# One weight sum per Strassen pair made by an accumulating DMA, splits of weights given priority, plain matmuls moved into the first pair, and y_diag issued ahead of the state update

## The chip, the cores and the metric

The kernel runs on one core of one Trainium2 chip. The metric is the device time of one execution in microseconds (us). The time before is the median of three runs. One further execution was taken with the hardware profiler; every share, row and duration below is from that one.

## The reference

One Mamba-2 layer on 512 tokens of 2048 channels, then a final RMSNorm. Everything is float32.

```python
hn   = rmsnorm(x, ln_g)                         # 512 x 2048
proj = hn @ w_in                                # 2048 x 10304: z 4096, xBC 6144, dt 64
xbc  = silu(causal_depthwise_conv(xBC))         # x 4096, B 8 x 128, C 8 x 128
dt   = softplus(dt + dt_bias);  a = -exp(a_log)
# per head (64 heads of 64 channels, 8 groups of 8 heads share B and C):
#   y_diag = (C B^T * decay) (x dt);  y_off = C state exp(cs);  state update
y    = (ssd_scan(x * dt, dt * a, B, C) + D * x) * silu(z)
out  = rmsnorm(x + rmsnorm(y) @ w_out, final_g)
```

## The kernel before

**Exact products from rounded parts.** TensorE's fast format is float32r. Each weight piece of 128 x 1024 floats (512 KB) is loaded raw and split by `split_piece` (L84): ScalarE casts it to a float32r part `hi` (L87), VectorE subtracts to make the rest `lo` (L88). The input `xh`, `xl` is split once. A product of k-slices is three matmuls: hi*xh, hi*xl, lo*xh (L635, L636, L637 for the in projection; L867, L868, L869 and L929, L930, L931 for the out projection).

**Plain part.** A head section computes dt from its weights, and eight 128-channel tiles (B0, C0 and the first x and z tiles) are multiplied in the plain way (`mm_k`, L198): 16 k-slices of three 512-column matmuls.

**Quads.** The other 36 pairs of tiles (`quads`: an x tile with its z tile, or a B tile with its C tile) go through `pair` (L639): one 2 x 2 Strassen-Winograd step with seven products of 24 matmuls of 128 x 256 each instead of eight. The weights of the products are, in the order in which a regular pair multiplies them, R11, T1, (T4 of the pair before), T2, R22, R21, T3. R11, R12, R21, R22 are quarters as loaded. T1 = R11 + another quarter and T3 = R12 + another are formed by an accumulating DMA on GpSimd's queue (`q_fetch`, L595, issue at L598): the second quarter is added into the raw piece in place. T2 = T1 + R22 and T4 = T2 + R21 are formed by VectorE in place (`q_add`, L604, 128 x 1024). The chain R11, T1, T2, T4 lives in one raw buffer of `ra` (three of them), R12 and T3 in the single `rb`, R22 and R21 in the two `rc`; the float32r parts rotate through three pairs of buffers, those of R11 have a pair of their own (`h1h`, `h1l`).

**The scan.** For each of 32 units (two heads), small groups of matmuls are inserted between the products: transposes (`u_xt`), the state update (`u_state`, L488), y_diag (`u_yd`, L502 and L506) and y_off (`u_yo`, L520). Between them ScalarE makes the decay exponentials (`u_decay`, L456 to L459), VectorE masks them (m, L461), the convolution runs on VectorE (L388, L391) with a SiLU on ScalarE (L394), and the unit's result is gated by z (xs, L523) and stored to DRAM (yscr, L524).

**What sets the order.** PE, SP and Pool run in an order fixed at build time: `ev` maps steps to lists of functions, `add` appends, and `run(step)` emits them. A product has four steps of six matmuls; a pair has 28 (`QS`). `q_events` (L610) places a pair's loads, splits, fetches and adds by offsets from its first step, so SP's queue holds the weight loads, the yscr stores and the decay loads csb in a fixed order. On VectorE and ScalarE a scheduler picks the order; work inside `urgent()` (high priority) goes ahead. In `split_piece` the split is urgent only for the out projection (`n >= len(quads)` in `q_split`).

**Out projection.** `blocks` alternates four plain blocks (512-column matmuls, `mm_o`) with two blocks of four Strassen pairs (`opair`, weights `wq`, products subtracted into the accumulator at L889 to L921), and ends with the RMSNorm. The first pair of the in projection and of each out block has no T4 of a pair before it: such a pair starts T1, R11 and then R22, T2, with four steps without matmuls. The loads of the first out pieces (rc, rb) stand in SP's queue behind the last pair's yscr store.

Of the kernel before, what the change touches and what calls it, by code (L numbers as in the profile page):

```python
# [1 line left out]

# [16 lines left out]
L = 512  # L19
# [15 lines left out]
def mamba_layer(ctx: ExitStack, tc: tile.TileContext, d: dict, out: bass.AP):  # L35
# [48 lines left out]
    def split_piece(raw, shape, pool, names=("hi", "lo"), bufs=None):  # L84
        hi = pool.tile(shape, F32R, name=names[0], bufs=bufs)
        lo = pool.tile(shape, F32R, name=names[1], bufs=bufs)
        S.copy(out=hi, in_=raw)  # L87
        V.tensor_tensor(out=lo, in0=raw, in1=hi, op=ALU.subtract)  # L88
        return hi, lo
# [26 lines left out]
    quads = seq[NPL // 2:]  # L116
    tile_of = {"z": 0, "x": 32, "B": 64, "C": 72}
    QS = 28
    at = {s: i * KT for i, s in enumerate(plain)}
    for i, pair in enumerate(quads):  # L120
        for s in pair:
            at[s] = NPL * KT + i * QS
    END = NPL * KT + len(quads) * QS
# [36 lines left out]
    def get_out(n, name="ra"):  # L160
        if n < len(wo_order) and n not in opieces:
            opieces[n] = split_piece(load_piece(wo_src(*wo_order[n]), OSH, name), OSH,
                                     *((op, ("oh", "ol")) if n % 4 == 3 else (wp,)))
# [475 lines left out]
    def pair(n, prev):  # L639

        b = NPL * KT + n * QS
# [7 lines left out]
        def first(step):  # L649
            product(s_, W("R11"), 11, True, step)  # L650
            with urgent():
                S.copy(out=A[:, lo_], in_=s_)

        def second(step):
            product(r_, W("T1"), 1, True, step)
            with urgent():
                S.copy(out=sn[:, 1, :], in_=r_)

        if prev:
            first(b)  # L660
            second(b + 4)
            prev(b + 8)
        else:
            second(b)
            first(b + 4)
            for i in range(8, 12):
                run(b + i)
        def third(step):
            product(r_, W("R22"), 4, False, step)

        def fourth(step):
            product(s_, W("T2"), 2, False, step)
            with urgent():
                S.copy(out=sn[:, 0, :], in_=s_)

        for f, step in zip((fourth, third) if prev else (third, fourth), (b + 12, b + 16)):
            f(step)
# [33 lines left out]
    ramp = [[66, 71, 63, 75, 87, 92], [56, 65, 50, 68, 86, 92]]
    for u in range(NU):
        w = ramp[u] if u < len(ramp) else [28, 42, 56, 65, 65, 71]
        for o, f in zip(w, (u_load, u_decay, u_xt, u_state, u_yd, u_yo)):
            add(at["x", u] + o, f, u)
    for n in range(len(quads)):
        q_events(n, NPL * KT + n * QS, n == len(quads) - 1, 0 if n else 14, lone=not n)
# [153 lines left out]
    def opair(i, s, b, prev):  # L871
# [9 lines left out]
        def first(step):  # L881
            oproduct(s_, i, W("R11"), 11, True, step)
            with urgent():
                S.copy(out=A0, in_=s_)

        def second(step):
            oproduct(r_, i, W("T1"), 1, True, step)
            with urgent():
                V.tensor_tensor(out=q1, in0=q1, in1=r_, op=ALU.subtract)  # L889

        if prev:
            first(b)
            second(b + 4)
            prev(b + 8)
        else:
            second(b)
            first(b + 4)
            for k in range(8, 12):
                run(b + k)
        def third(step):  # L900
            oproduct(r_, i, W("R22"), 4, False, step)
            V.tensor_tensor(out=q0, in0=q0, in1=r_, op=ALU.subtract)

        def fourth(step):
            oproduct(s_, i, W("T2"), 2, False, step)
            with urgent():
                V.tensor_tensor(out=q0, in0=q0, in1=s_, op=ALU.subtract)

        for f, at_ in zip((fourth, third) if prev else (third, fourth), (b + 12, b + 16)):
            f(at_)  # L910
# [90 lines left out]
    for kb, blk in enumerate(blocks[:-1]):  # L1001
        if type(blk) is tuple:
# [5 lines left out]
            continue  # L1008
        end = n0 + n_pieces(blk) + (n_pieces(blocks[kb + 1]) if kb + 2 < len(blocks) else 0)
        for s, pairs in blk:  # L1010
            ps = [None] * NC
            for p in pairs:
# [26 lines left out]
                if n0 == 7:  # L1039
# [5 lines left out]
                    nc.sync.dma_start(fg, d["fg"].partition_broadcast(P))  # L1045

# [65 lines left out]
```

## Time and profile before

| what | value |
|---|---|
| median of three runs | 1290.69 us (1289.58 to 1293.99) |
| profiled execution, its own time | 1295.7 us |
| profiled execution, span on the core | 1294.0 us |
| mean granted TensorE clock | 0.991 |
| GpSimd (POOL) busy | 77.5 us, 6% |
| HBM traffic | 211.52 MB read, 12.78 MB written |

How to read what the prediction quotes: PE is TensorE's matmuls, PEld its weight loads, DVE VectorE, ACT ScalarE, SPq and POOLq the queues of SyncE and GpSimd. "out<-in" names the tiles by the program's names. In a group, "x44 | 53.7, 1220 | 0.0" is 44 instructions, 53.7 us busy, 1220 ns each, and no idle time of the engine just ahead of them. In the list of waits, "5.6, 9, 1.5" is 5.6 us in total, 9 times, the longest 1.5 us. In a stretch of the timeline a row begins with its start and its length in us. PE's pace of matmuls is modelled at the end of each, so its busy time shows the stretches in which it had nothing to run and not how well it runs.

### The profile page before, as it was taken

Reading aid. Unit: us, or ns where it says so; the run is one execution under the profiler, and the core shown is the slowest. Engines: PE = TensorE matmul, PEld = TensorE weight load, DVE = VectorE, ACT = ScalarE, POOL = GpSimd, SP = SyncE. Lnnn points to the kernel's source line nnn. Section 1 sums busy time; section 2 is a strip of 40 time slices with the busy share of each in tenths; the row PEclk is TensorE's granted clock in tenths of the full one; section 3 lists DMA queues with packets and bytes.
Section 4 is the critical chain, followed back from the end, with each engine's and each line's share of the span. In section 5 each row is a group of like instructions: output and inputs, shape, how many; then the busy total and the mean of one; then the engine's idle time right before and its main releaser. Section 6 shows DMA issues by size and latency. Waiting matters only on the chain.

```text
span 1294.0 us, 24519 instructions
## 1 busy us (share of the span) xinstructions
PE 1252.1 (97%) x9932; PEld 1192.9 (92%) x9932; DVE 1084.3 (84%) x1449; ACT 826.6 (64%) x1357; POOL 77.5 (6%) x99
## 2 busy tenths in 40 slices
PE   8989899999999999999999999999999899999997
PEld 8989899999999999999999999999988899899885
DVE  5796988988989898998889899889857877887865
ACT  7667667677666757767685867778666445434433
POOL 0000001010000101010100001000000000000000
PEclk9989999999999999999999999999999999999999
DMA  9546657585676667667667677766637576647612
GB/s 356 179 141 172 162 161 174 143 215 142 192 197 174 159 169 183 164 176 199 162 161 195 151 188 171 212 155 154 185 105 258 146 199 199 197 119 229 183 57 98
DMA packets 70194, 225.90 MB, mean 175 GB/s; under 512 B 8384, under 2 KB 12800, under 8 KB 69952
## 3 DMA queue, kind: packets, MB, share of 16 engines
q1 hardware_dynamic: 56688, 176.34, 40.2%
q0 software_dynamic: 12672, 46.14, 22.1%
q8 instruction: 78, 1.28, 0.4%
q10 hardware_dynamic: 720, 1.84, 0.4%
q14 instruction: 36, 0.29, 0.1%
HBM read 211.52 MB, written 12.78 MB: 173 GB/s over the span
## 4 chain that ended last, share of the span: by engine, by line
PE 74%; DVE 11%; DMA 7%; issue 4%; ACT 3%; SPq 0%; POOL 0%; DVEq 0%; ACTq 0%; POOLq 0%
PE S L637 7%; PE S L635 7%; PE S L636 7%; PE mm L635 5%; PE mm L636 4%; PE R L635 4%; PE mm L637 4%; PE R L636 4%; PE R L637 4%; DVE lo L88 3%; PE mm L929 3%; PE mm L931 3%; PE mm L930 3%; PE yd L502 2%; PE mm L867 2%
## 5 line engine op out<-in xcount | busy, mean ns | idle before, releaser
L87 ACT CAST hi<-ra 128x1024 fp32r<-128x1024 f32 x150 | 154.7, 1046 | 159.5 <-DVE ra L604 72.9
L88 DVE TENSOR_TENSOR lo<-ra,hi 128x1024 fp32r<-128x1024 f32 x150 | 181.3, 1221 | 24.2 <-ACT hi L87 24.1
L635 PE MATMUL mm<-xh,hi 128*128 128x256 f32 x576 | 163.6, 284 | 0.0
L637 PE MATMUL mm<-xh,lo 128*128 128x256 f32 x576 | 160.6, 279 | 0.6 <-DVE lo L88 0.6
L636 PE MATMUL mm<-xl,hi 128*128 128x256 f32 x576 | 160.4, 278 | 0.0
L637 PE MATMUL R<-s,lo 128*128 128x256 f32 x576 | 160.3, 278 | 0.1
L635 PE MATMUL R<-s,hi 128*128 128x256 f32 x576 | 160.2, 278 | 0.0
L636 PE MATMUL R<-s,hi 128*128 128x256 f32 x576 | 160.2, 278 | 0.0
L88 DVE TENSOR_TENSOR lo<-rc,hi 128x1024 fp32r<-128x1024 f32 x94 | 114.9, 1223 | 28.5 <-ACT hi L87 28.1
L87 ACT CAST hi<-rc 128x1024 fp32r<-128x1024 f32 x94 | 98.4, 1047 | 50.8 <-issue 29.1
L604 DVE TENSOR_TENSOR ra<-ra,rc 128x1024 f32<-128x1024 f32 x88 | 107.7, 1224 | 13.3 <-DMA rc<-in_wi 11.8
L635 PEld LDWEIGHTS mm<-xh,hi 128*128 128x128 f32 x576 | 108.1, 188 | 5.2 <-issue 5.0
L637 PEld LDWEIGHTS mm<-xh,lo 128*128 128x128 f32 x576 | 109.2, 190 | 0.8 <-DVE lo L88 0.8
L637 PEld LDWEIGHTS R<-s,lo 128*128 128x128 f32 x576 | 109.1, 189 | 0.3 <-DVE lo L88 0.3
L635 PEld LDWEIGHTS R<-s,hi 128*128 128x128 f32 x576 | 108.2, 188 | 0.0
L636 PEld LDWEIGHTS mm<-xl,hi 128*128 128x128 f32 x576 | 108.2, 188 | 0.0
L636 PEld LDWEIGHTS R<-s,hi 128*128 128x128 f32 x576 | 108.1, 188 | 0.0
L637 PE MATMUL S<-xh,lo 128*128 128x256 f32 x288 | 83.5, 290 | 5.6 <-DVE lo L88 5.6
L635 PE MATMUL S<-xh,h1h 128*128 128x256 f32 x288 | 83.4, 290 | 1.0 <-DVE xr L398 1.0
L635 PE MATMUL S<-xh,hi 128*128 128x256 f32 x288 | 81.3, 282 | 2.2 <-ACT xh L577 1.3
L636 PE MATMUL S<-xl,hi 128*128 128x256 f32 x288 | 81.2, 282 | 0.7 <-DVE xl L578 0.7
L636 PE MATMUL S<-xl,h1h 128*128 128x256 f32 x288 | 80.8, 280 | 0.0
(452 smaller groups left out, 3940.8 us busy)
## 6 DMA issues: line engine op xcount, KB each, us to landing
rc<-in_wi SPq DMA_DIRECT2D x76, 512.0 KB, 5.9
ra<-in_wi SPq DMA_DIRECT2D x42, 512.0 KB, 6.2
rb<-in_wi SPq DMA_DIRECT2D x40, 512.0 KB, 6.9
ra<-in_wi POOLq DMA_DIRECT2D x36, 512.0 KB, 6.3
rb<-in_wi POOLq DMA_DIRECT2D x36, 512.0 KB, 5.9
csb<-cscr SPq DMA_DIRECT2D x32, 512.0 KB, 8.0
ra<-in_wo SPq DMA_DIRECT2D x26, 512.0 KB, 5.4
yscr<-xs SPq DMA_DIRECT2D x32, 256.0 KB, 2.6
```

The lines of the kernel that those rows point to most:

```text
L87: S.copy(out=hi, in_=raw)
L88: V.tensor_tensor(out=lo, in0=raw, in1=hi, op=ALU.subtract)
L502: T.matmul(pyd[r, i, :], x[:, 2 * i, hh, :], m[:, i, hh::4, :], start=i == 0, stop=False, skip_group_check=True)
L604: V.tensor_tensor(out=raw, in0=raw, in1=qs[n][other], op=ALU.add)
L635: T.matmul(ps, hi[:, k, :], ah, start=first and k == 0, stop=False, skip_group_check=True)
L636: T.matmul(ps, hi[:, k, :], al, start=False, stop=False, skip_group_check=True)
L637: T.matmul(ps, lo[:, k, :], ah, start=False, stop=k == KH - 1, skip_group_check=True)
L867: T.matmul(ps[:, t, :], yh[:, k, tt], hi[:, k, :], start=st, stop=False, skip_group_check=True)
L929: T.matmul(ps, yh, hi, start=first and k == 0, stop=False)
L930: T.matmul(ps, yh, lo, start=False, stop=False)
L931: T.matmul(ps, yl, hi, start=False, stop=last and k == 1)
```

## The change

1. `split_piece` makes every cast and every subtraction urgent; before, only those of the out projection's pairs.
2. T4 = T2 + R21 is formed by a third accumulating DMA (`q_fetch` at step 8 of the pair, from DRAM into the raw `ra` buffer that holds T2) and no longer by VectorE (`q_add` at step 12). The raw piece R21 is still loaded and split for its own product. 44 of the 88 instructions of L604 go, and GpSimd's queue has 132 accumulating DMAs in place of 88.
3. The last four k-slices of the last plain tile are multiplied as the `prev` of the first pair, which then has the order of all others (`QB`, the step at which the pairs start, is four less). Likewise the last two token tiles of the plain out block ahead of each Strassen block run as the `prev` of that block's first pair (`bridge`, `tail`).
4. Within a step all units' loads, decays and transposes are emitted first, then y_diag, then the B and C work of the groups, then the state update and y_off. So y_diag stands ahead of the state update where both are at step 65.
5. Which out pieces take the buffers `oh`, `ol` (`get_out`), and the steps at which the first Strassen out block's y is loaded and formed, are shifted by a few.

```diff
     def split_piece(raw, shape, pool, names=("hi", "lo"), bufs=None):
         hi = pool.tile(shape, F32R, name=names[0], bufs=bufs)
         lo = pool.tile(shape, F32R, name=names[1], bufs=bufs)
-        S.copy(out=hi, in_=raw)
-        V.tensor_tensor(out=lo, in0=raw, in1=hi, op=ALU.subtract)
+        with urgent():
+            S.copy(out=hi, in_=raw)
+            V.tensor_tensor(out=lo, in0=raw, in1=hi, op=ALU.subtract)
         return hi, lo
 
...
+    QB = NPL * KT - 4
...
-    END = NPL * KT + len(quads) * QS
+            at[s] = QB + i * QS
+    END = QB + len(quads) * QS
     WSH = [P, 8, P]
     OSH = [P, 2, L]
...
+        late -= 4 if type(blocks[min(i + 1, len(blocks) - 1)]) is tuple else 0
...
-                                     *((op, ("oh", "ol")) if n % 4 == 3 else (wp,)))
+                                     *((op, ("oh", "ol")) if n and n % 4 == 0 else (wp,)))
...
-        with urgent() if n >= len(quads) else ExitStack():
-            qs[n, f] = split_piece(raw, WSH if n < len(quads) else QSH, wp, *((("h1h", "h1l"), 1) if own else ()))
+        qs[n, f] = split_piece(raw, WSH if n < len(quads) else QSH, wp, *((("h1h", "h1l"), 1) if own else ()))
...
-    def q_events(n, b, last, e=0, t1=0, lone=False):
+    def q_events(n, b, last, e=0):
         for o, f, a in ((-38 - e, q_load, ("R11", 0, 0, "ra")), (-23 - e, q_split, ("R11", True)),
-                        (-23 - e, q_fetch, ("T1", "R11", 0, 1)), (-3 - e // 2 - t1, q_split, ("T1",)),
+                        (-23 - e, q_fetch, ("T1", "R11", 0, 1)), (-3 - e // 2, q_split, ("T1",)),
                         (-12 - e // 2, q_load, ("R22", 1, 1, "rc")), (1 - e // 2, q_add, ("T2", "T1", "R22")),
-                        *(((5, q_split, ("R22",)), (9, q_split, ("T2",))) if lone else
-                          ((5, q_split, ("T2",)), (9, q_split, ("R22",)))),
-                        (-8, q_load, ("R21", 1, 0, "rc")), (12, q_add, ("T4", "T2", "R21")),
+                        (5, q_split, ("T2",)), (9, q_split, ("R22",)),
+                        (-8, q_load, ("R21", 1, 0, "rc")), (8, q_fetch, ("T4", "T2", 1, 0)),
                         (13, q_split, ("R21",)),
                         (-7, q_load, ("R12", 0, 1, "rb")), (-7, q_fetch, ("T3", "R12", 1, 1)),
                         (17, q_split, ("T3",)), (23 if last else 29, q_split, ("T4",))):
...
+        product(s_, W("R11"), 11, True, b)
+        with urgent():
+            S.copy(out=A[:, lo_], in_=s_)
+        product(r_, W("T1"), 1, True, b + 4)
+        with urgent():
+            S.copy(out=sn[:, 1, :], in_=r_)
+        prev(b + 8)
+        product(s_, W("T2"), 2, False, b + 12)
+        with urgent():
+            S.copy(out=sn[:, 0, :], in_=s_)
+        product(r_, W("R22"), 4, False, b + 16)
...
+    ramp = [[66, 71, 63, 75, 87, 92], [56, 65, 50, 68, 86, 92]]
+    steps = [ramp[u] if u < len(ramp) else [28, 42, 56, 65, 65, 71] for u in range(NU)]
+
+    def add_units(*kinds):
+        for u in range(NU):
+            for i, f in kinds:
+                add(at["x", u] + steps[u][i], f, u)
+
+    add_units((0, u_load), (1, u_decay), (2, u_xt))
+    add_units((4, u_yd))
     for g in range(1, G):
         add(at["B", g] + (30 if ("B", g) in plain else 93), g_bt, g)
         for i in range(2):
...
+    add_units((3, u_state), (5, u_yo))
...
+    def prev(step):
+        for i in range(4):
+            run(step + i)
+            mm_k(ps, pieces[2 * NPL - 1], 4 + i, KT - 4 + i)
+        finish(NPL - 1, ps)
+
...
-                add(base[i] - ((50, 32), (54, 32))[m][j], y_fetch, m, j)
-                add(base[i] - ((39, 24), (47, 24))[m][j], y_forms, m, j)
+                add(base[i] - ((48, 30), (54, 32))[m][j], y_fetch, m, j)
+                add(base[i] - ((36, 23), (47, 24))[m][j], y_forms, m, j)
...
+        def tail(ps, w, y, t, s, first, step):
+            for k in range(2):
+                run(step + k)
+            mm_o(ps, w, y, t, first, True)
+            a = acc[:, t, s * L:(s + 1) * L]
+            with urgent():
+                V.tensor_tensor(out=a, in0=ps, in1=a, op=ALU.add)
+
+        bridge = []
+        n_end = n0 + n_pieces(blk)
...
+                    if type(blocks[kb + 1]) is tuple and s == 3 and n0 + 1 == n_end and t > 1:
+                        bridge.append(partial(tail, ps[t], opieces[n0], ys[p], t, s, p == pairs[0]))
+                        continue
...
+        if bridge:
+            def prev(step, parts=bridge):
+                for i, f in enumerate(parts):
+                    f(step + 2 * i)
```

The rows below are lists of instructions in program order for one engine, before and after.

**VectorE, late in a regular pair** (the pair of the x tile whose convolution makes xs_6524; lo_6538 is of R21, lo_6593 of T3, lo_6653 of the next T1, lo_6703 of T4). Before:

```order
L391 SCALAR_TENSOR_TENSOR xs_6524<-xr_112,par_98,xs_6524 128x512
L522 TENSOR_TENSOR xs_6232<-xs_6232,ecs_6114 128x256
L391 SCALAR_TENSOR_TENSOR xs_6524<-xr_112,par_98,xs_6524 128x512
L523 TENSOR_TENSOR xs_6232<-xs_6232,z_5853 128x512
L461 TENSOR_TENSOR m_6547<-m_6547,cbm_6391 128x1536
L88 TENSOR_TENSOR lo_6593<-rb_6333,hi_6592 128x1024
L529 TENSOR_TENSOR sx_113<-sx_113,z_5853 128x512
L679 TENSOR_TENSOR z_6389<-R_6387,sn_6388 128x256
L88 TENSOR_TENSOR lo_6653<-ra_6310,hi_6652 128x1024
L88 TENSOR_TENSOR lo_6703<-ra_6022,hi_6702 128x1024
```

After:

```order
L395 SCALAR_TENSOR_TENSOR xs_6525<-xr_112,par_98,xs_6525 128x512
L525 TENSOR_TENSOR ecs_6114<-yo_6495,ecs_6114 128x256
L395 SCALAR_TENSOR_TENSOR xs_6525<-xr_112,par_98,xs_6525 128x512
L526 TENSOR_TENSOR xs_6233<-xs_6233,ecs_6114 128x256
L90 TENSOR_TENSOR lo_6593<-rb_6333,hi_6592 128x1024
L395 SCALAR_TENSOR_TENSOR xs_6525<-xr_112,par_98,xs_6525 128x512
L465 TENSOR_TENSOR m_6547<-m_6547,cbm_6405 128x1536
L90 TENSOR_TENSOR lo_6653<-ra_6310,hi_6652 128x1024
L527 TENSOR_TENSOR xs_6233<-xs_6233,z_5853 128x512
L90 TENSOR_TENSOR lo_6703<-ra_6022,hi_6702 128x1024
```

The subtraction for T3 (lo<-rb) has moved ahead of the last convolution tap and of m; the gating xs_6233<-xs_6233,z_5853, which the yscr store waits for, now stands behind lo<-rb, m and the next T1's lo<-ra.

**VectorE, end of the last pair of the in projection** (lo_11304 is of the last T3, lo_11322 of the first out piece). Before:

```order
L391 SCALAR_TENSOR_TENSOR xs_11237<-xr_112,par_98,xs_11237 128x512
L523 TENSOR_TENSOR xs_10953<-xs_10953,z_10535 128x512
L461 TENSOR_TENSOR m_11260<-m_11260,cbm_10537 128x1536
L88 TENSOR_TENSOR lo_11304<-rb_11052,hi_11303 128x1024
L529 TENSOR_TENSOR sx_113<-sx_113,z_10535 128x512
L679 TENSOR_TENSOR z_11108<-R_11106,sn_11107 128x256
```

After:

```order
L90 TENSOR_TENSOR lo_11304<-rb_11052,hi_11303 128x1024
L395 SCALAR_TENSOR_TENSOR xs_11238<-xr_112,par_98,xs_11238 128x512
L526 TENSOR_TENSOR xs_10954<-xs_10954,ecs_10840 128x256
L395 SCALAR_TENSOR_TENSOR xs_11238<-xr_112,par_98,xs_11238 128x512
L465 TENSOR_TENSOR m_11260<-m_11260,cbm_10551 128x1536
L527 TENSOR_TENSOR xs_10954<-xs_10954,z_10535 128x512
```

The gating xs<-xs,z of the unit stood ahead of m and lo<-rb, and now stands behind both.

**VectorE, first Strassen pair of the out projection** (ra_11874 before and ra_11796 after hold T1, then T2; L952 and L930 add x; L907 and L888 subtract the T2 product). Before:

```order
L604 TENSOR_TENSOR ra_11874<-ra_11874,rc_12011 128x1024
L952 SCALAR_TENSOR_TENSOR acc_11459<-xt_12100,rms_11395,acc_11459 128x512
L88 TENSOR_TENSOR h1l_12114<-ra_12021,h1h_12113 128x1024
L88 TENSOR_TENSOR lo_12138<-ra_11874,hi_12137 128x1024
L88 TENSOR_TENSOR lo_12149<-rc_12031,hi_12148 128x1024
L88 TENSOR_TENSOR lo_12180<-rb_12033,hi_12179 128x1024
L604 TENSOR_TENSOR ra_11874<-ra_11874,rc_12031 128x1024
L902 TENSOR_TENSOR acc_11459<-acc_11459,mm_12072 128x2x256
L88 TENSOR_TENSOR lo_12244<-ra_12021,hi_12243 128x1024
L907 TENSOR_TENSOR acc_11459<-acc_11459,mm_12071 128x2x256
```

After (L993 adds the plain products that now run as `prev`):

```order
L993 TENSOR_TENSOR acc_11459<-mm_12055,acc_11459 128x512
L607 TENSOR_TENSOR ra_11796<-ra_11796,rc_11995 128x1024
L993 TENSOR_TENSOR acc_11459<-mm_12056,acc_11459 128x512
L930 SCALAR_TENSOR_TENSOR acc_11459<-xt_12086,rms_11395,acc_11459 128x512
L90 TENSOR_TENSOR lo_12096<-ra_11796,hi_12095 128x1024
L90 TENSOR_TENSOR lo_12125<-rc_11995,hi_12124 128x1024
L90 TENSOR_TENSOR lo_12149<-rc_12015,hi_12148 128x1024
L886 TENSOR_TENSOR acc_11459<-acc_11459,mm_12057 128x2x256
L90 TENSOR_TENSOR lo_12180<-rb_12017,hi_12179 128x1024
L888 TENSOR_TENSOR acc_11459<-acc_11459,mm_12058 128x2x256
L90 TENSOR_TENSOR lo_12244<-ra_12005,hi_12243 128x1024
L607 TENSOR_TENSOR ra_12005<-ra_12005,rc_12171 128x1024
```

The add that forms T2 now stands between the two evacuations of the moved plain products; the second add, T4 = T2 + R21, is gone from in front of the subtractions, and the split of R22 (lo_12125), which stood ahead of these rows before, now comes behind that of T2 (lo_12096).

On ScalarE the cast for T3 (hi<-rb) stood behind the last decay exponentials (L458, L459) of the unit and now stands ahead of them; where B and C tiles are made, more changes between functions follow, so that the program has 83 loads of ScalarE's function tables instead of 71. SP's queue holds the same loads and stores in the same order through all regular pairs; GpSimd's queue goes from ra, rb in turn to ra, ra, rb.

More of the change, by code (lines that the diff above doesn't have):

```diff
@@ L1 @@
 from contextlib import ExitStack
+from functools import partial
 import numpy as np
@@ L121, in mamba_layer @@
         for s in pair:
-            at[s] = NPL * KT + i * QS
-    END = NPL * KT + len(quads) * QS
+            at[s] = QB + i * QS
+    END = QB + len(quads) * QS
     WSH = [P, 8, P]
@@ L639, in pair @@
     def pair(n, prev):
-        b = NPL * KT + n * QS
+        b = QB + n * QS
         (kp, ip), (kq, iq) = quads[n]
@@ L647, in pair @@
         A = ps_mm.tile([P, L], F32, name="mm")
[L649 to L677, printed above, removed]
+        product(s_, W("R11"), 11, True, b)
[9 more added lines that the diff above has]
+        product(r_, W("R22"), 4, False, b + 16)
         with urgent():
@@ L710, in mamba_layer @@
             add(at["x", 4 * g] + 28, g_cb, g, i)
[L711 to L715, printed above, removed]
+    add_units((3, u_state), (5, u_yo))
     for n in range(len(quads)):
-        q_events(n, NPL * KT + n * QS, n == len(quads) - 1, 0 if n else 14, lone=not n)
+        q_events(n, QB + n * QS, n == len(quads) - 1, 0 if n else 14)
     for i in range(4):
@@ L790, in mamba_layer @@
         ps = None
-        for k in range(KT):
+        for k in range(KT if n < NPL - 1 else KT - 4):
             if k % 8 == 0:
@@ L802, in mamba_layer @@
             st["x0"] = ps
-        else:
+        elif n < NPL - 1:
             finish(n, ps)
-    prev = None
+    def prev(step):
[3 more added lines that the diff above has]
+        finish(NPL - 1, ps)
     for n in range(len(quads)):
@@ L879, in opair @@
         A0 = ps_mm.tile([P, 2, LH], F32, name="mm")
[L881 to L910, printed above, removed]
+        oproduct(s_, i, W("R11"), 11, True, b)
+        with urgent():
+            S.copy(out=A0, in_=s_)
+        oproduct(r_, i, W("T1"), 1, True, b + 4)
+        with urgent():
+            V.tensor_tensor(out=q1, in0=q1, in1=r_, op=ALU.subtract)
+        prev(b + 8)
+        oproduct(s_, i, W("T2"), 2, False, b + 12)
+        with urgent():
+            V.tensor_tensor(out=q0, in0=q0, in1=s_, op=ALU.subtract)
+        oproduct(r_, i, W("R22"), 4, False, b + 16)
+        V.tensor_tensor(out=q0, in0=q0, in1=r_, op=ALU.subtract)
         oproduct(A0, i, W("R21"), 12, False, b + 20)
@@ L965, in mamba_layer @@
             for s in range(4):
-                q_events(len(quads) + 4 * m + s, base[i] + s * QS, s == 3, 0, 3 if s == 0 else 0, s == 0)
+                q_events(len(quads) + 4 * m + s, base[i] + s * QS, s == 3)
             for j in range(2):
-                add(base[i] - ((50, 32), (54, 32))[m][j], y_fetch, m, j)
-                add(base[i] - ((39, 24), (47, 24))[m][j], y_forms, m, j)
+                add(base[i] - ((48, 30), (54, 32))[m][j], y_fetch, m, j)
+                add(base[i] - ((36, 23), (47, 24))[m][j], y_forms, m, j)
             m += 1
@@ L1008, in mamba_layer @@
             continue
+        def tail(ps, w, y, t, s, first, step):
[3 more added lines that the diff above has]
+            a = acc[:, t, s * L:(s + 1) * L]
+            with urgent():
+                V.tensor_tensor(out=a, in0=ps, in1=a, op=ALU.add)
+        bridge = []
+        n_end = n0 + n_pieces(blk)
         end = n0 + n_pieces(blk) + (n_pieces(blocks[kb + 1]) if kb + 2 < len(blocks) else 0)
```

## Prediction

> **What bounds the kernel now.** I read the profile's page, then a stretch of the regular pairs, then the list of what TensorE waits for, and last the rows at each wait. The page:
>
> ```profile
> PE 1252.1 (97%) x9932; PEld 1192.9 (92%) x9932; DVE 1084.3 (84%) x1449; ACT 826.6 (64%) x1357; POOL 77.5 (6%) x99
> ...
> q1 hardware_dynamic: 56688, 176.34, 40.2%
> q0 software_dynamic: 12672, 46.14, 22.1%
> ...
> PE 74%; DVE 11%; DMA 7%; issue 4%; ACT 3%; SPq 0%; POOL 0%; DVEq 0%; ACTq 0%; POOLq 0%
> ```
>
> TensorE carries 74% of the chain that ended last and is busy for 97% of the span. The stretch from 200 to 920 us, nearly all of the regular pairs:
>
> ```profile
> core 0: us, PE busy (x) PEld busy (x) DVE busy (x) ACT busy (x) POOL busy (x), PEclk, DMA share, GB/s
> 200.00:920.00 720.00, 715.18 (x6203) 696.94 (x6202) 644.81 (x828) 514.16 (x882) 54.95 (x64) 1.00 0.68 175
> ```
>
> TensorE is idle there for 720.00 - 715.18 = 4.8 us, at the full clock. The change takes no matmul away, so it can give at most TensorE's waits. These are all:
>
> ```profile
> PE yo L198 <- ACT xh L181: 6.1, 1, 6.1
> PE S L637 <- DVE lo L88: 5.6, 9, 1.5
> PE S L198 <- DVE lo L88: 4.0, 1, 4.0
> PE mm L867 <- DVE acc L907: 2.5, 1, 2.5
> PE mm L869 <- DVE lo L88: 1.8, 2, 1.4
> PE mm L867 <- ACT mm L916: 1.7, 1, 1.7
> PE mm L867 <- DVE acc L889: 1.7, 1, 1.7
> PE S L635 <- ACT xh L577: 1.3, 1, 1.3
> PE mm L930 <- DVE lo L88: 1.2, 1, 1.2
> PE tr L373 <- DVE xd L476: 1.0, 1, 1.0
> PE S L635 <- DVE xr L398: 1.0, 1, 1.0
> PE S L635 <- ACT hi L87: 0.9, 1, 0.9
> PE mm L867 <- ACT hi L87: 0.9, 1, 0.9
> PE S L636 <- DVE xl L578: 0.7, 1, 0.7
> PE mm L637 <- DVE lo L88: 0.6, 1, 0.6
> PE tr L473 <- DVE win L366: 0.6, 1, 0.6
> PE S L930 <- DVE lo L88: 0.5, 1, 0.5
> ```
>
> They make 32.1 us. The first, 6.1 us in the head, is out of the change's reach, so 26 us are in play, 2% of the span. The ninefold 5.6 us is T3's `lo` part arriving late in the pairs; L198's 4.0 us is a plain tile whose `lo` part is late; L867 and L869 are in the Strassen blocks of the out projection.
>
> **The change part by part.** VectorE's and the queue's durations:
>
> ```profile
> L604 DVE TENSOR_TENSOR ra<-ra,rc 128x1024 f32<-128x1024 f32 x88 | 107.7, 1224 | 13.3 <-DMA rc<-in_wi 11.8
> ...
> L88 DVE TENSOR_TENSOR lo<-rb,hi 128x1024 fp32r<-128x1024 f32 x50 | 61.1, 1222 | 2.9 <-ACT hi L87 2.9
> L461 DVE TENSOR_TENSOR m<-m,cbm 128x1536 f32<-128x1536 f32 x32 | 56.1, 1754 | 3.7 <-ACT m L459 3.6
> ...
> L523 DVE TENSOR_TENSOR xs<-xs,z 128x512 f32<-128x512 f32 x32 | 22.0, 688 | 0.1
> ```
> ```profile
> rb<-in_wi SPq DMA_DIRECT2D x40, 512.0 KB, 6.9
> ra<-in_wi POOLq DMA_DIRECT2D x36, 512.0 KB, 6.3
> rb<-in_wi POOLq DMA_DIRECT2D x36, 512.0 KB, 5.9
> ```
>
> *T4 by DMA.* VectorE loses 44 x 1.224 = 53.9 us of work; as it is no bound by itself (84%), that shortens nothing directly. GpSimd's queue gains 44 transfers. The 88 of now take 22.1% of 16 engines, so one takes 0.221 x 1294 / 88 = 3.25 us of all 16, and 44 more raise the queues' share from 62% to 73%. T4's sum lands about 6.3 us after its issue (the row of ra), and its split stands 21 steps behind the issue (8 to 29). A step is six matmuls of 715.18 / 6203 = 0.115 us, 0.69 us; 21 x 0.69 = 14.5 us cover the 6.3, and T4's own arrival costs 0. Without that cover it would cost up to 6.3 us a pair. What it can cost is the later landing of other transfers: from 0 to 3.25 us each, taken up under the rivals.
>
> *Splits ahead, in the regular pairs.* T3's `lo` now runs ahead of m (1.754). Nine waits of 5.6 us came from its place behind m and the gating; the longest is 1.5 us, less than m alone. So in 200 to 920 us the 4.8 us may go. Against it stands what the gating pays: it moves behind lo<-rb, m and T1's lo<-ra, 1.22 + 1.75 + 1.22 = 4.2 us later, and on SP's queue the next pair's loads wait behind its store:
>
> ```profile
> 566.70 0.33 SPq L524 DMA_DIRECT2D yscr<-xs  x1
> ...
> 589.23 0.33 SPq L524 DMA_DIRECT2D yscr<-xs  x1
> ...
> 591.09 0.38 SPq L81 DMA_DIRECT2D rb<-in_wi  x1
> ```
>
> R12's load issues 1.9 us behind the store. The reserve of T3's sum shows between the issue of its accumulation and its cast, in the pair between those two stores:
>
> ```profile
> 577.47 0.88 POOL L598 DMA_DIRECT2D rb<-in_wi  x1 [19.23 <-DMA rb<-in_wi]
> ```
> ```profile
> 586.44 1.05 ACT L87 CAST hi<-rb 128x1024 fp32r<-128x1024 f32 x1 [2.00 <-PE S L636]
> ```
>
> 577.47 + 5.9 = 583.4, 3.1 us ahead of the cast. A shift of 4.2 us overruns that by 1.1 us, while `lo` behind the cast no longer waits for m's 1.75; where the reserve is as thin as here the two about balance, and elsewhere the waits go. So I count 3.5 us of the 4.8; the bounds are +4.8 and the rival's loss.
>
> *ScalarE's tables.* Twelve more table loads:
>
> ```profile
> L458 ACT ACTIVATE m<-csb,nwl 128x128 f32<-128x128 f32 x128 | 50.5, 394 | 0.4
> ...
> L458 ACT ACT_TABLE_LOAD x31 | 39.8, 1283 | 0.2
> ```
>
> 12 x 1.283 = 15.4 us on an engine that is idle for 36% of the span, hidden: 0. The Trainium skill, "ScalarE: Activation LUTs", What ACT_TABLE_LOAD costs, gives the same 1283 ns but adds a drain of about 1380 ns, 2.66 us for a switch; by it ScalarE would pay 32 us and the loop of the first rival would be some 1.4 us longer for each load in it. The rows show 0.2 us of idle time ahead of all 31 loads together and 0.4 us ahead of the 128 exponentials, so no drain is to be seen here.
>
> *First pair.* T1 ahead of R11 and the four empty steps go. R11 of the second pair (L398 1.0), the cast and `lo` of its T3 (0.9 and 0.8, the latter within the 5.6) and R21's `lo` (L637 of mm, 0.6) come in time: 3.3 us. L577's 1.3 and the 0.7 of `xl` behind it stay, as their chain on VectorE isn't moved: +3.3, from +1.3 (two of the four gone) to +4.6 (L577's too).
>
> *Plain tile.* lo<-rb goes ahead of dt's chain on VectorE, so L198's 4.0 goes; but that chain, which ends in the first decays and y_diag, starts later by the two splits put ahead of it, 2 x 1.22, and more where it waits for a cast. L373's 1.0 shows that TensorE already waits for it. I take the two as equal: 0, from -1.5 to +4.0.
>
> *yd ahead of the state update.* The same matmuls in another order: 0. No row shows the other order; one matmul's 0.115 us lost or won at each of 30 units bounds it at 3.5 us either way.
>
> *First out piece.* Its load rc<-in_wo stands behind the last pair's store:
>
> ```profile
> 924.02 0.33 SPq L524 DMA_DIRECT2D yscr<-xs  x1
> 924.44 0.38 SPq L81 DMA_DIRECT2D rc<-in_wo  x1
> ```
> ```profile
> 923.30 0.69 DVE L523 TENSOR_TENSOR xs<-xs,z 128x512 f32<-128x512 f32 x1
> ```
>
> The store follows the gating by 0.03 us. The gating moves behind lo<-rb and m, 1.22 + 1.75 = 3.0 us, and there is no reserve: TensorE waits for this piece's `lo` already (S L930, 0.5). So -3.0, from 0 (if the gating's wait is hidden) to -3.5. This is the new wait of which I am surest.
>
> *Strassen blocks of the out projection.* In the first pair, L907's 2.5 us came from a subtraction queued behind a `lo` that waited for its load; the second add in front is gone: +2.5. The 1.4 and 0.9 of T2's `lo` and cast stay, since the add that makes T2 is queued behind the evacuation of a moved plain product: 0. In the second block L889's 1.7 goes with the order T1, R11: +1.7. L916's 1.7, L930's 1.2 and the rest of L869 stay. Together +4.2, from 0 to 9.
>
> Sum: 3.5 + 3.3 + 0 + 0 - 3.0 + 4.2 = 8.0 us. The profiled execution took 1295.7 us and its span 1294.0, 5.0 and 3.3 above the median of 1290.69; I carry that distance over unchanged. So the span would be 1286.0 and the median 1290.7 - 8.0 = **1282.7 us**. About 0.3%, 3.9 us, is what a measurement of this kernel can tell from no change.
>
> **Rivals.** *The loop through SP's queue closes (slower).* From store to store: 1.9 to R12's load, 6.9 to its landing, 0.7 to GpSimd's issue (an estimate from GpSimd's 0.88 us of issue), 5.9 to T3's sum, 1.05 cast, 1.22 `lo`, 1.75 m, 1.22 T1's `lo`, 0.69 gating: 21.3 us, against 589.23 - 566.70 = 22.5 between stores now. It holds with 1.2 us to spare, if no landing is later. T4's transfers can make landings later by up to 3.25 us. Over the four linked pairs of a group (32 stores in 36 pairs, the chain broken once a group) lateness adds up to 4 x (d - 1.2); it decides once that exceeds the 3.1 us of reserve, d = 2.0. At d = 2.6, 4 x 1.4 - 3.1 = 2.5 us in each of 7 groups is 17.5, and the 3.5 gained is lost: 1282.7 + 21.0 = 1303.7 us. For it: a store follows its gating within 0.03 us already, so SP waits there now, and the reserve is thin. Against: DMA is busy for 68%, and T4's sums are issued in mid pair, away from the loads. The Trainium skill, "DMA: Bandwidth & Descriptors", Issuing engines are not separate DMA queues, says that DMAs of all issuers interleave on the same 16 engines; so by it GpSimd's third sum is no free lane, and it speaks for this rival. The trace doesn't contradict it, with a median of 6.9 us for rb's load on SP beside 5.9 for the sum on GpSimd. Chance 0.18.
>
> *The waits only move (no change).* Regular pairs give 0, the first pair 1.3, the out blocks 4.2, less the 3.0 of the first out piece: 2.5 us, 1288.2. For it: VectorE does the same splits, ordered otherwise. Chance 0.15.
>
> *Nearly all goes (faster still).* The plain tile's 4.0 stays gained, the first out piece's 3.0 is hidden, T2's 2.3 goes too: 9.3 more, 1273.4. For it: VectorE has 53.9 us less to do. Chance 0.15.
>
> **How the numbers follow.** Forecast 0.52, the rivals 0.18, 0.15, 0.15. Faster by over 0.3% is below 1286.8: forecast less 0.02 for its upper end, and the last rival, 0.65. Slower is above 1294.6: 0.18. The same: 0.17. The forecast's own range, by the bounds of its terms mixed, is 1276 to 1288. For 8 in 10 I go down to 1271, past the last rival, and up to 1296, past the one without change and into the start of the slow one.
>
> **What would show it.** Right: waits of S on `lo` gone from 200 to 920 us with TensorE idle for under 2 us; no wait on L907's successor; a wait of some 3.5 us for the first out piece's `lo`, its load issued 3 us later behind yscr; VectorE at about 1030 us. Wrong: yscr stores more than 22.5 us apart and T3's cast waiting for rb's DMA (the first rival); L198's wait gone with nothing behind it (the last one).

## The result and the profile after

The changed kernel took 1346.37 us (median of four runs, 1342.22 to 1350.8) beside 1292.21 us of the kernel before in the same comparisons: a ratio of 1.0421, 95% interval 1.0373 to 1.047. It is 54 us slower where 8 us faster were forecast. Its profiled execution has a span of 1347.9 us.

The page after, with the same lines as before: TensorE's idle share has risen from 3% to 6%, and of the chain that ended last TensorE has 35% where it had 74%; 37% are now DMAs, of `ra`, `rb` and csb above all.

```profile
PE 1269.1 (94%) x9932; PEld 1200.3 (89%) x9932; DVE 1044.2 (77%) x1405; ACT 844.0 (63%) x1369; POOL 117.3 (9%) x143
...
q1 hardware_dynamic: 56688, 176.34, 37.9%
q0 software_dynamic: 19008, 69.21, 29.9%
...
DMA 37%; PE 35%; DVE 13%; ACT 8%; issue 5%; POOL 1%; SPq 1%; POOLq 0%; DVEq 0%; ACTq 0%
DMA ra<-in_wi 15%; DMA rb<-in_wi 11%; DMA csb<-cscr 5%; DVE lo L90 5%; PE mm L907 4%; PE mm L908 4%; PE mm L909 4%; ACT hi L89 3%; PE mm L863 2%; PE mm L865 2%; PE mm L864 2%; DMA yr<-yscr 2%; DMA ra<-in_wo 1%; PE S L638 1%; DVE m L465 1%
```

The stretch from 200 to 920 us: TensorE is idle for 29.3 us where it was for 4.8, and does 5920 matmuls in it where it did 6203.

```profile
core 0: us, PE busy (x) PEld busy (x) DVE busy (x) ACT busy (x) POOL busy (x), PEclk, DMA share, GB/s
200.00:920.00 720.00, 690.72 (x5920) 667.78 (x5920) 588.40 (x759) 505.50 (x850) 81.53 (x93) 0.99 0.75 189
```

What TensorE waits for, in us, times and the longest. The ninefold wait for T3's `lo` (S L637, 5.6 us before) is down to 0.8 (S L639, 3 times), as forecast; in its place stand waits for ScalarE's copy of T3's product (mm L668), which T4's product is added to, for m, for y_off's operand and for the first out piece (S L907).

```profile
PE mm L637 <- ACT mm L668: 12.6, 7, 2.7
PE yd L506 <- DVE m L465: 10.3, 7, 1.9
PE yo L202 <- ACT xh L185: 6.0, 1, 6.0
PE mm L863 <- ACT mm L894: 6.0, 4, 1.9
PE S L907 <- ACT hi L89: 5.6, 1, 5.6
PE S L637 <- ACT xh L581: 4.0, 1, 4.0
PE yo L522 <- DVE stsl L408: 3.8, 5, 1.0
PE S L202 <- ACT hi L89: 3.6, 1, 3.6
...
PE S L639 <- DVE lo L90: 0.8, 3, 0.5
```

The starts of TensorE's rows divide the run into stages: until the third pair's R11, the 34 pairs from there to the first matmul of the out projection, and the rest.

| kernel | until pair 3 | 34 pairs | out part | span |
|---|---|---|---|---|
| before | 170.3 | 759.5 | 364.2 | 1294.0 |
| after | 172.5 | 799.0 | 376.5 | 1347.9 |

39.5 of the 53.9 us are in the second stage, 12.3 in the out part. The wait for the first out piece (5.6 us) falls at the end of the second stage, so some 34 us are the pairs' own.

**The loop.** One turn of it, between two yscr stores of regular pairs. SP's queue: the store, three loads, R12's load, and csb.

```profile
542.79 0.33 SPq L528 DMA_DIRECT2D yscr<-xs  x1
543.23 0.38 SPq L82 DMA_DIRECT2D rc<-in_wi  x1
...
544.67 0.37 SPq L82 DMA_DIRECT2D rb<-in_wi  x1
545.14 0.70 SPq L444 DMA_DIRECT2D csb<-cscr  x1
...
567.15 0.33 SPq L528 DMA_DIRECT2D yscr<-xs  x1
```

GpSimd's queue: T3's sum waits for R12's load, and the two sums into `ra`, the next T1's and T4's, stand behind it. The row names what VectorE had finished last (h1l, at 553.55); the chain that ended last has R12's landing there, at 544.67 + 8.74 = 553.41.

```profile
554.08 0.86 POOL L601 DMA_DIRECT2D rb<-in_wi  x1 [22.32 <-DVE h1l L90]
554.71 2.02 POOL L601 DMA_DIRECT2D ra<-in_wi  x2
```
```profile
544.67 8.74 DMA rb<-in_wi
```

ScalarE: the decays wait for csb, and with the casts among them take until 563.2; the cast of T1 waits for its sum.

```profile
554.87 0.40 ACT L460 ACTIVATE m<-csb,cs 128x128 f32<-128x128 f32 x1 [1.26 <-DMA csb<-cscr]
...
562.14 1.05 ACT L463 ACTIVATE m<-m 128x1024 f32<-128x1024 f32 x1
563.57 1.05 ACT L89 CAST hi<-ra 128x1024 fp32r<-128x1024 f32 x1 [0.38 <-DMA ra<-in_wi]
```

VectorE: m, then T1's `lo`, then the gating, at whose end the next store issues.

```profile
563.63 1.75 DVE L465 TENSOR_TENSOR m<-m,cbm 128x1536 f32<-128x1536 f32 x1
565.30 1.22 DVE L90 TENSOR_TENSOR lo<-ra,hi 128x1024 fp32r<-128x1024 f32 x1
566.44 0.68 DVE L527 TENSOR_TENSOR xs<-xs,z 128x512 f32<-128x512 f32 x1
```

So a store releases the loads, the loads release (after some 9 us) two chains, T3's and T1's sums and the decays with m, and both end ahead of the next store's gating on VectorE. A turn takes 567.15 - 542.79 = 24.4 us, and TensorE needs some 22 (a kernel below takes 742.9 us for the 34 pairs, 21.9 each). The second chain sets this turn; the first, whose cast ends at 564.62, would end 0.7 us sooner. Turns are not alike: this one and the next three take 24.4, 24.8, 21.0 and, with a B and C pair in it, 44.8 us, 115.0 for five pairs; in the kernel before the same five take 23.4, 22.4, 22.5 and 42.8, 111.1. So the lateness gathers over a group of units and does not show in every turn.

### The profile page after: what moved, and what is told of

Its sections match the earlier page's. It is cut to its first block, busy times and chain, and to the rows that moved or that the text cites. A ratio compares the mean times of both kernels' runs of the same rounds, so it can differ in the third digit from the quotient of the medians.

```text
span 1347.9 us, 24633 instructions
## 1 busy us (share of the span) xinstructions
PE 1269.1 (94%) x9932; PEld 1200.3 (89%) x9932; DVE 1044.2 (77%) x1405; ACT 844.0 (63%) x1369; POOL 117.3 (9%) x143
## 4 chain that ended last, share of the span: by engine, by line
DMA 37%; PE 35%; DVE 13%; ACT 8%; issue 5%; POOL 1%; SPq 1%; POOLq 0%; DVEq 0%; ACTq 0%
DMA ra<-in_wi 15%; DMA rb<-in_wi 11%; DMA csb<-cscr 5%; DVE lo L90 5%; PE mm L907 4%; PE mm L908 4%; PE mm L909 4%; ACT hi L89 3%; PE mm L863 2%; PE mm L865 2%; PE mm L864 2%; DMA yr<-yscr 2%; DMA ra<-in_wo 1%; PE S L638 1%; DVE m L465 1%
## 5 line engine op out<-in xcount | busy, mean ns | idle before, releaser
L89 ACT CAST hi<-ra 128x1024 fp32r<-128x1024 f32 x153 | 160.0, 1047 | 171.9 <-DVE ra L607 86.4
L90 DVE TENSOR_TENSOR lo<-ra,hi 128x1024 fp32r<-128x1024 f32 x153 | 186.8, 1221 | 81.3 <-ACT hi L89 79.9
L637 PE MATMUL mm<-xh,hi 128*128 128x256 f32 x576 | 163.9, 285 | 12.6 <-ACT mm L668 12.6
L639 PE MATMUL mm<-xh,lo 128*128 128x256 f32 x576 | 160.4, 279 | 0.5 <-DVE lo L90 0.5
L637 PE MATMUL R<-s,hi 128*128 128x256 f32 x576 | 160.0, 278 | 0.2 <-DVE z L663 0.2
L639 PE MATMUL R<-s,lo 128*128 128x256 f32 x576 | 159.9, 278 | 0.0
L90 DVE TENSOR_TENSOR lo<-rc,hi 128x1024 fp32r<-128x1024 f32 x92 | 112.4, 1223 | 29.5 <-ACT hi L89 29.3
L637 PEld LDWEIGHTS mm<-xh,hi 128*128 128x128 f32 x576 | 109.0, 189 | 14.2 <-ACT mm L668 14.0
L639 PEld LDWEIGHTS mm<-xh,lo 128*128 128x128 f32 x576 | 109.0, 189 | 0.7 <-DVE lo L90 0.7
L637 PEld LDWEIGHTS R<-s,hi 128*128 128x128 f32 x576 | 108.3, 188 | 0.6 <-DVE z L663 0.6
L639 PEld LDWEIGHTS R<-s,lo 128*128 128x128 f32 x576 | 108.5, 188 | 0.2 <-DVE lo L90 0.2
L601 POOL DMA_DIRECT2D rb<-in_wi x36 | 31.0, 861 | 714.8 <-DMA rb<-in_wi 310.9
L637 PE MATMUL S<-xh,hi 128*128 128x256 f32 x288 | 81.2, 282 | 5.5 <-ACT xh L581 4.0
L637 PE MATMUL S<-xh,h1h 128*128 128x256 f32 x288 | 83.4, 290 | 0.0
L639 PE MATMUL S<-xh,lo 128*128 128x256 f32 x288 | 82.1, 285 | 0.9 <-DVE lo L90 0.8
L607 DVE TENSOR_TENSOR ra<-ra,rc 128x1024 f32<-128x1024 f32 x44 | 53.8, 1224 | 37.0 <-DMA rc<-in_wi 33.7
```

Source lines behind the costliest of these rows:

```text
L601: nc.gpsimd.dma_start(raw, q_src(n, half, tile_)[0], accum_op=ALU.add)
L607: V.tensor_tensor(out=raw, in0=raw, in1=qs[n][other], op=ALU.add)
L637: T.matmul(ps, hi[:, k, :], ah, start=first and k == 0, stop=False, skip_group_check=True)
L639: T.matmul(ps, lo[:, k, :], ah, start=False, stop=k == KH - 1, skip_group_check=True)
```

## The experiments

Three theories stood after the result. **L**: the loop just shown. **D**: the load of 44 more transfers on the DMA engines. **C**: urgent casts that wait for their DMA hold back ScalarE's evacuations of PSUM.

**One part undone, one part alone.**

```diff
# undo_t4, on the changed kernel
-(8, q_fetch, ("T4", "T2", 1, 0))
+(12, q_add, ("T4", "T2", "R21"))
# undo_urgent, on the changed kernel
-        with urgent():
-            S.copy(out=hi, in_=raw)
-            V.tensor_tensor(out=lo, in0=raw, in1=hi, op=ALU.subtract)
+        S.copy(out=hi, in_=raw)
+        V.tensor_tensor(out=lo, in0=raw, in1=hi, op=ALU.subtract)
...
+        with urgent() if n >= len(quads) else ExitStack():
# t4_alone, on the kernel before
-(12, q_add, ("T4", "T2", "R21"))
+(10 if lone else 8, q_fetch, ("T4", "T2", 1, 0))
# urgent_alone, on the kernel before: the two lines of split_piece under urgent()
```

undo_t4. 

> The changed kernel with T4 formed by VectorE again (q_add at step 12), all else as changed. Theory L (a loop through SP's queue: the gating stands behind the next T1's lo, that T1's sum stands on GpSimd's queue behind T3's, and T3's load stands on SP's queue behind the store that the gating releases): the loop stays, but T1's sum lands some 2 us sooner without T4's beside it, so part of the loss goes: 1305 to 1325 us. Theory D (the load of 44 more transfers on the DMA engines): all of the loss goes, 1280 to 1295. Theory C (urgent casts that wait for their DMA hold back ScalarE's evacuations of PSUM): most of the loss stays, 1325 to 1345.

undo_urgent. 

> The changed kernel with splits urgent only for the out projection's pairs, as before; T4 still by DMA. Theory L: the gating no longer waits for lo<-rb and T1's lo, the loop opens, 1280 to 1300 us. Theory D: the loss stays, 1330 to 1346. Theory C: 1280 to 1300, as L.

t4_alone. 

> The kernel before with only T4 formed by an accumulating DMA (issue step 8, in the pairs without a T4 before them step 10). Theory L: the gating is where it was, so no loop closes: 1285 to 1300 us. Theory D: the loss is here, 1320 to 1345. Theory C: 1285 to 1300.

urgent_alone. 

> The kernel before with only the splits urgent, T4 by VectorE. Theory L: the gating stands behind T1's lo, the loop is near TensorE's own 22.4 us a pair: 1295 to 1320 us, stores 22.5 to 23.5 us apart. Theory D: no loss, 1283 to 1293. Theory C: the whole loss without T4's DMA, 1325 to 1345.

Measured: undo_t4 1332.0 us (ratio to before 1.0278, 1.0234 to 1.0323), undo_urgent 1324.57 (1.0231, 1.0191 to 1.0271), t4_alone 1306.58 (1.0104, 1.0072 to 1.0136), urgent_alone 1340.5 (1.034, 1.0293 to 1.0386). D falls as the main cause: the DMA alone costs 12 us and the priority alone 46. But t4_alone's 1306.58 lies between D's numbers and those of the other two, so the DMA is not free either. undo_t4 and urgent_alone are slower than L's numbers and lie in C's, undo_urgent lies far from both. If L holds, the loop closes without T4's DMA too; urgent_alone's stores are 23.6 us apart.

```profile
570.62 0.33 SPq L525 DMA_DIRECT2D yscr<-xs  x1
...
594.20 0.33 SPq L525 DMA_DIRECT2D yscr<-xs  x1
```

undo_urgent came out 24 us above the range that both L and C gave it. Its waits are others, for T3's `lo` again:

```profile
PE S L639 <- DVE lo L89: 16.2, 15, 1.9
```

In its list of VectorE's instructions m stands ahead of the gating and of T3's `lo`. The order of events (part 4 of the change) was the suspect:

```diff
# undo_urgent_yd: undo_urgent, and events added as before
-    add_units((0, u_load), (1, u_decay), (2, u_xt))
-    add_units((4, u_yd))
...
+        for o, f in zip(w, (u_load, u_decay, u_xt, u_state, u_yd, u_yo)):
+            add(at["x", u] + o, f, u)
```

> The changed kernel without the splits' priority and with the old order of events within a step. Without the priority alone it took 1324.6 us, 18 us more than T4's DMA alone on the kernel before, and VectorE had m ahead of the gating and of T3's lo. If the order of events did that (the scheduler ranks what is emitted first higher), it comes back: 1298 to 1308. If it is the moved plain work: 1318 to 1326.

Measured: 1314.41 us (1.0145, 1.0122 to 1.0169), between the two expectations. The old order brings back 10 us, in the profiled executions 7 in the pairs; VectorE's list has the gating first again. Of the 16.4 us by which its span is still longer than before, 10.7 are in the out part (below).

**Cutting the loop, at two places and on one engine.** L and C part here.

```diff
# gate_urgent, on the changed kernel (u_yo)
+        with urgent():
             V.tensor_tensor(out=ecs, in0=pyo, in1=ecs, op=ALU.mult)
             V.tensor_tensor(out=y[:, 2 * P:L], in0=y[:, 2 * P:L], in1=ecs, op=ALU.add)
             V.tensor_tensor(out=y, in0=y, in1=z, op=ALU.mult)
# store_later, on the changed kernel (u_yo)
-        nc.sync.dma_start(yscr[u // UPG][:, u % UPG, :], y)
+        store = partial(nc.sync.dma_start, yscr[u // UPG][:, u % UPG, :], y)
+        if 1 < u < NU - 2:
+            add(at["x", u] + steps[u][5] + 15, store)
+        else:
+            store()
# hi_only, on the changed kernel (split_piece)
         with urgent():
             S.copy(out=hi, in_=raw)
-            V.tensor_tensor(out=lo, in0=raw, in1=hi, op=ALU.subtract)
+        with urgent() if names[0] == "oh" or shape[1] != 8 else ExitStack():
+            V.tensor_tensor(out=lo, in0=raw, in1=hi, op=ALU.subtract)
# t4_in, on the changed kernel
+((8, q_fetch, ("T4", "T2", 1, 0)) if n < len(quads) else (12, q_add, ("T4", "T2", "R21")))
```

gate_urgent. 

> The changed kernel with the three VectorE steps of the gating (y_off times its decay, the sum, times z) urgent too: the gating then stands ahead of the last convolution tap, of m and of T1's lo, behind lo<-rb alone. Theory L (the loop from the gating over SP's queue to the next pair's loads and decays and back to m and T1's lo, which stand ahead of the gating): the loop is cut, most of the 39 us lost in the regular pairs comes back, 1305 to 1322 us. Theory C (casts that wait for their DMA hold back ScalarE): nothing moves there, 1335 to 1346.

store_later. 

> The changed kernel with each unit's yscr store issued 15 steps later, behind the next pair's weight loads and decay load in SP's queue; VectorE's and ScalarE's priorities as changed. Theory L: the gating releases nothing but the store, the loop is cut, 1305 to 1325 us. If the loop only runs over the decay chain on VectorE and ScalarE and not over SP's queue, or by theory C: 1335 to 1346.

hi_only. 

> The changed kernel with ScalarE's casts urgent and VectorE's subtractions for the in projection at their old priority, so that the gating stands ahead of lo<-rb, m and T1's lo again while ScalarE keeps the order of the change. Theory L: 1305 to 1322 us. Theory C: the loss stays, 1335 to 1346.

t4_in. 

> The changed kernel with T4 of the out projection's pairs formed by VectorE, in the in projection by DMA. If the 12 us lost from the first out piece on come from T4's sums there: 1332 to 1338 us. If they come from the moved plain work or from lateness that the pairs hand over: 1343 to 1349.

Measured: gate_urgent 1295.38 us (1.0011, 0.9996 to 1.0027), store_later 1297.37 (1.0016, 0.999 to 1.0042), hi_only 1291.18 (0.9971, 0.9953 to 0.9989), t4_in 1341.04 (1.0387, 1.0333 to 1.0442). Each of the first three takes back about 50 us, more than L's numbers said. C falls, as ScalarE's urgent casts are in all three. store_later keeps VectorE's order of the change, gating last, and moves nothing but the issue of a 256 KB store; in its SP queue the store now has no load right behind it:

```profile
542.69 1.75 DVE L465 TENSOR_TENSOR m<-m,cbm 128x1536 f32<-128x1536 f32 x1
544.36 1.22 DVE L90 TENSOR_TENSOR lo<-ra,hi 128x1024 fp32r<-128x1024 f32 x1
545.50 0.68 DVE L527 TENSOR_TENSOR xs<-xs,z 128x512 f32<-128x512 f32 x1
```
```profile
546.21 0.33 SPq L718 DMA_DIRECT2D yscr<-xs  x1
555.92 0.34 SPq L82 DMA_DIRECT2D rc<-in_wi  x1
556.36 0.73 SPq L82 DMA_DIRECT2D ra<-in_wi  x1
560.98 0.33 SPq L82 DMA_DIRECT2D rc<-in_wi  x1
564.10 0.33 SPq L82 DMA_DIRECT2D rb<-in_wi  x1
```

That shows the loop to run over SP's queue; since the store releases both chains, no run tells them apart. t4_in differs by 5 us from the changed kernel and lies between its two expectations; its interval overlaps the changed kernel's, so by itself it tells little.

**A version from the parts.** hi_only had 14 us less than before in the pairs and 10.6 more in the out part.

```diff
# hi_t4in: hi_only, with T4 as in t4_in
# hi_no_t4: hi_only, with T4 as in undo_t4
# casts_t4in_alone, on the kernel before: S.copy in split_piece urgent, T4 by DMA for n < len(quads)
```

hi_t4in. 

> The changed kernel with only ScalarE's casts urgent (VectorE's subtractions for the in projection at their old priority) and T4 of the out projection's pairs by VectorE. Theory L has left 14 us of gain in the regular pairs and 10 us of loss from the first out piece on; if that loss is from T4's sums in the out projection's pairs, which are shorter and whose casts then wait for them, the time is 1278 to 1285 us; if it is from the moved plain work, 1288 to 1292.

hi_no_t4. 

> The changed kernel with only ScalarE's casts urgent and every T4 by VectorE, as before. Tells what T4's DMA is worth in the regular pairs once the loop is open: if VectorE's 44 x 1.22 us matter there, 3 to 8 us slower than with T4 by DMA in the in projection (1283 to 1292); if TensorE was never waiting for them, the same as that kernel (1278 to 1285).

casts_t4in_alone. 

> The kernel before with ScalarE's casts urgent and T4 of the in projection by DMA, and nothing else: no plain work in first pairs, the old order of events. If the first pair's part of the forecast holds (3.3 us there, 1.7 us in the second out block), this is 4 to 6 us slower than the same with them, 1283 to 1290; if they bring nothing, 1278 to 1284.

Measured: hi_t4in 1278.6 us (0.9876, 0.9849 to 0.9903), hi_no_t4 1293.26 (0.9988, 0.9969 to 1.0007), casts_t4in_alone 1284.98 (0.9919, 0.9902 to 0.9936). hi_t4in is faster than both kernels. hi_no_t4 is 1 us above the upper of its two ranges and level with the kernel before; casts_t4in_alone is 6.4 us slower than hi_t4in, as its first expectation had it. hi_t4in's stretch from 200 to 920 us, of which the last 10 us are already in the out part, and where TensorE is idle for 2.1 us:

```profile
200.00:920.00 720.00, 717.88 (x6302) 699.52 (x6302) 623.49 (x812) 523.36 (x897) 82.50 (x95) 1.00 0.80 202
```

The stages of all runs, from one profiled execution each:

| kernel | 34 pairs | out part |
|---|---|---|
| t4_alone | 763.3 | 366.9 |
| urgent_alone | 796.8 | 367.0 |
| undo_t4 | 788.7 | 365.5 |
| undo_urgent | 773.5 | 378.2 |
| undo_urgent_yd | 766.6 | 374.9 |
| t4_in | 793.5 | 370.7 |
| gate_urgent | 750.3 | 370.3 |
| store_later | 751.3 | 375.2 |
| hi_only | 745.3 | 374.8 |
| hi_t4in | 742.9 | 364.4 |
| hi_no_t4 | 758.1 | 361.1 |
| casts_t4in_alone | 745.0 | 365.8 |

T4's DMA is worth 758.1 - 742.9 = 15 us in the pairs once the loop is open and the casts go first; without it TensorE still waits there for T3's `lo`, for 8.7 us in all:

```profile
PE S L640 <- DVE lo L91: 8.7, 6, 1.9
```

With T4 by DMA and the old priorities (t4_alone) the pairs gain nothing: 763.3 beside 759.5. In the out part T4's DMA costs 10.4 us (374.8 beside 364.4). Only in the kernels with the moved plain work (part 3 of the change) is the out part long: t4_alone has T4 by DMA there as well and 366.9. These kernels all have part 5 too, the shifted buffers and steps of the out projection, and no run has one without the other. Of where these 10 us go the trace shows a part: TensorE's waits for casts and for the copy ahead of T4's product, and ScalarE's casts that wait for the sums, in hi_only,

```profile
PE mm L864 <- ACT hi L89: 4.4, 2, 2.4
PE mm L864 <- ACT mm L895: 3.9, 2, 2.6
```
```profile
ACT hi L89 <- DMA ra<-in_wq: 10.1, 3, 5.1
```

and in hi_t4in, where no cast waits for such a sum:

```profile
PE mm L864 <- ACT mm L895: 2.2, 1, 2.2
PE mm L864 <- ACT hi L89: 1.9, 1, 1.9
```

That T4's DMA costs more there together with parts 3 and 5 is shown by the pairing of runs (10.4 us beside 366.9 - 364.2 = 2.7 without them), with one profiled execution of each; that it is the moved plain work and not part 5, and by which wait, is only argued.

## Why the prediction was wrong, point by point

- **Regular pairs, +3.5 forecast, some -34 measured** (39.5 in the stage, less the out piece's wait). This is the step that failed: the gating's shift of 4.2 us was set against a reserve of 3.1 us and against m's 1.75, "the two about balance", as if it ended there and did not come back through the store. The T3 waits went as forecast, and the first rival was the right mechanism: the gating behind T1's `lo`, the loads behind the store, one loop. It was given a chance of 0.18, a turn of 21.3 us and a condition (landings over 2.0 us later) that wasn't needed. Two links were missing from the turn. The next T1's sum stands behind T3's on GpSimd's queue, so VectorE's T1 `lo` is not free to run when its cast is emitted: the issue at 554.71 (0.63 us behind T3's) to the cast at 563.57 is 8.9 us. And m hangs on csb, which is loaded behind the same store: 545.14 to 554.87 from its issue to the first decay, 8.3 us of decays and casts, 1.75 of m. I counted m's 1.75 us and left out what m waits for. urgent_alone shows that T4's transfers were not needed for it, since it loses 37.3 us in the second stage without them.
- **The price.** I let lateness run up only past a reserve of 3.1 us and took 21 us. With a turn longer than TensorE's own pair a reserve only delays the loss: 799.0 / 34 = 23.5 us a pair beside 22.3.
- **T4 by DMA.** "Shortens nothing directly" held for the old priorities (3.8 us slower in the pairs in t4_alone) and failed with urgent casts, where it is worth 15 us. Its effect on landings was in the forecast range: 9.2 us for sums into `ra` beside 6.3, 8.1 for R12's loads beside 6.9.

```profile
ra<-in_wi POOLq DMA_DIRECT2D x72, 512.0 KB, 9.2
...
rb<-in_wi SPq DMA_DIRECT2D x40, 512.0 KB, 8.1
...
csb<-cscr SPq DMA_DIRECT2D x32, 512.0 KB, 9.0
```

- **First out piece, -3.0 forecast.** Right in its mechanism: the store (965.94) follows the gating, the load is behind it, and TensorE waits 5.6 us (S L907) where it waited 0.5. The size was 5.1 us, not 3.0.

```profile
965.94 0.33 SPq L528 DMA_DIRECT2D yscr<-xs  x1
966.36 0.38 SPq L82 DMA_DIRECT2D rc<-in_wo  x1
```

- **First pair and plain tile, +3.3 and 0.** Until the third pair's R11 the changed kernel is 2.2 us later, not 3.3 earlier. The wait for `xh` (S L637) grew from 1.3 to 4.0 us, and the plain tile's wait moved from `lo` (4.0) to the cast (3.6). hi_only, which differs from the changed kernel in the subtractions' priority alone, reaches that point at 167.4 us, so the urgent subtractions took 5.1 us there. hi_t4in reaches it at 167.0, 3.3 earlier than before, the forecast's number, but in part by luck: casts_t4in_alone, with the casts and T4's DMA and without the moved work and the new order, is there at 171.9, 1.6 later than before. So the moved work with the new order gave 4.9 us, and the casts with T4's DMA took 1.6; each is from one profiled execution.
- **Out blocks, +4.2.** The wait for L907's successor went; 12.3 us were lost in the part as a whole. T4's DMA together with parts 3 and 5 of the change was not seen as a cost there.
- **ScalarE's tables and the order of y_diag, 0 each.** store_later keeps all 83 table loads and is level with the kernel before, so they cost nothing that shows there. The order of events cost 10 us in undo_urgent (1324.57 beside 1314.41), through VectorE's order and not through the 0.115 us a unit that I had bounded: the events of a step also rank the scheduler's work.
- **The clock.** The mean granted clock fell from 0.991 to 0.979. 1347.9 x 0.021 = 28.3 us are lost to it, beside 1294.0 x 0.009 = 11.6 before. So by this estimate up to 16.7 of the 53.9 us went to the clock, a term that the forecast didn't have. It is an upper bound: 4 us of the longest halved stretch (below) passed while TensorE waited anyway, and where the loop sets the pace a slower matmul may cost nothing.

## What to carry to other kernels

When a priority moves an instruction on one engine, follow what that instruction releases on a queue with a fixed order, through everything that stands behind it there, until you are back at the instruction that now goes first: if the turn is longer than the bound's own period, the loop is the new bound, and no share of busy time names it. Include what each operand in the turn waits for, its loads and the sums queued ahead of it, and not only its own duration. Then test by moving the release (a store a few steps later in its queue) before giving up the change: here the whole change with only the casts urgent and T4's DMA in the in projection alone gave 1.2%, and these two on the kernel before, without its other parts, 0.8%.

## What the runs showed of the hardware

In these traces waits cost TensorE more than their length, through the granted clock. Two stretches of the changed kernel around the wait for the first out piece, with the clock behind the busy times:

```profile
900.00:970.00 70.00, 64.61 (x557) 61.43 (x556) 55.75 (x74) 50.10 (x89) 7.03 (x8) 0.98 0.74 183
970.00:1060.00 90.00, 84.81 (x415) 69.36 (x415) 57.66 (x85) 52.64 (x83) 2.58 (x3) 0.94 0.53 167
```

and the same two places of the kernel before, where the wait was 0.5 us:

```profile
860.00:930.00 70.00, 70.00 (x604) 67.91 (x602) 61.80 (x82) 51.17 (x91) 4.32 (x5) 1.00 0.67 173
930.00:1020.00 90.00, 87.20 (x473) 73.79 (x472) 67.00 (x98) 53.21 (x85) 2.56 (x3) 1.00 0.57 179
```

In the traces' clock records behind this column the clock is halved for stretches of 3.4 to 10.2 us, 56.2 us of the span in the changed kernel, 22.4 in the kernel before and 24.4 in hi_t4in; the longest, 10.2 us, begins at 967.5, 1.7 us into the wait for the first out piece. The Trainium skill, "TensorE: Matmul & The Clock Gate", HAM oscillation — how this bites in real kernels, tells of the same return to half clock and puts the rule at gaps over some 3.4 us. Here shorter ones were followed by it too. In the changed kernel a halved stretch begins at 1063.0 us, at the end of a wait of 2.04 us, and one at 1141.6, 1.5 us behind a wait of 1.92; behind a wait of 2.68 us that ends at 388.33 there is none before 516.9.

```profile
1063.10 0.58 PE L863 MATMUL mm<-hi,f2h 128*128 128x256 f32 x1 [2.04 <-ACT hi L89]
388.33 0.39 PE L637 MATMUL mm<-xh,hi 128*128 128x256 f32 x1 [2.68 <-ACT mm L668]
```

So the length of one wait does not decide it in these traces; what does is not shown.
